# Four-column-quarter fp32 matmuls for the second half of a modulation, and a later place for two steps at the entry of a feed-forward loop

## The chip, the cores and the metric

One core of a Trainium2 chip runs the program. TensorE (PE in the profile, its weight loads PEld) multiplies, VectorE (DVE), ScalarE (ACT) and GpSimd (POOL) work element by element, SyncE (SP) issues the transfers from and to HBM. The metric is the device time in microseconds of one execution; lower is better. The program is laid out by a tile framework at build: it allots buffers and fixes the order of instructions on each engine, and at run time each engine goes through its own list in that order and waits on semaphores.

## The reference, cut to what matters

One transformer block on x of 512 tokens by 1024, in fp32, with a mixer of three kinds of heads:

```python
mod = jax.nn.silu(c) @ w_ada[l] + b_ada[l]                    # 1024 -> 6 * 1024
sh1, sc1, g1, sh2, sc2, g2 = jnp.split(mod[:, None, :], 6, axis=-1)
hn = _rms(x, norm1_g[l]) * (1 + sc1) + sh1
y = _mixer(hn, w_in[l], ...)                                  # projections, forget attention, mLSTM, block attention
x = x + g1 * (y @ w_out[l])
hn = _rms(x, norm2_g[l]) * (1 + sc2) + sh2
gate, up = jnp.split(hn @ w_gate_up[l], 2, axis=-1)
x = x + g2 * ((jax.nn.silu(gate) * up) @ w_down[l])
```

The modulation is a product of one row with a matrix of 1024 by 6144. Its "second half" below are the four parts that are not needed for the first norm: g1, sc2, sh2 and g2, 1024 columns each.

## The kernel before, in words

The first stage (to about 60 us) makes sc1 and sh1, normalizes x, transposes it and starts the first projection. The mixer stage follows (about 60 to 300 us): 70 steps, each a half row of projection products, between which a planner's queue puts the parts of the attention heads by due times written in the code. Then comes the rest of the output projection with norm 2, then the feed-forward loop (blocks of 256 of the 2816 hidden columns, q = 1 to 10, each in seven phases of a Strassen-like scheme), and the down projection in two halves.

*The modulation.* `cs` holds silu(c), 128 partitions by 8. `ada_half` (line 595) makes 512 columns: for each of 8 k, SyncE loads a tile of 128x512 of `w_ada` (tag `ast`, three buffers), and VectorE multiplies it by the column `cs[:, k]` and adds it to `acc`. The sum over partitions is left to a product with ones: `ada_row` (line 612, for g1 and g2) multiplies a full matrix of ones with `acc` into a PSUM bank of tag "t" (there are two of these) and ScalarE copies the bank to `g1b`; `ada_col` (line 619, for sc2 and sh2) multiplies four blocks of `acc` with a column of ones. g1, sc2 and sh2 are pulled by `next(ada)` once a step from step 12 on (line 1009); g2 by `next(ada2)` at every second product of the down projection (line 1352). In the profile the tiles are called g10s, g11s, sc20s, sc21s, sh20s, sh21s, g20s, g21s (loads) and g, sc, sh (sums), and g1p, g2p, sc2p, sh2p (banks).

*The entry to the feed-forward loop.* `plain(hb)` (line 1248) multiplies block 0 of the hidden columns without the scheme, for the two halves of the tokens; its bank is `fp`. `plain_glu(hb)` (line 1265) makes silu of the gate half on ScalarE (`fps`) and the product with the up half on VectorE (`A`). `operands` (line 1082) makes the scheme's operands from the normalized tokens: `operand` (line 1073) rounds a tile on ScalarE (`...h`) and subtracts on VectorE (`...l`). The last of them, s4, is a12 - a11, written over a12 (`hf<-hf`), then rounded and split (`os40h`, `os40l`, `os41h`, `os41l`). Behind these and both `plain_glu` calls stands the loop: `prepare(q, 6)` (line 1159) runs `sums` (line 1145), VectorE's sums and differences of raw weights (`r`, `r1t`), and `split` (line 1139) makes the pair `fw16h` and `fw16l` for the first product, `f1A`. The phases run in the order 1, 2, 6, 5, 7, 4, 3; for q = 1 the first two are done early, and s4 is used in phase 3. SyncE's order is the program's from line 1272 on.

Of the kernel before, what the change touches and what calls it, by code (L numbers as in the profile page):

```python
# [8 lines left out]
F32 = mybir.dt.float32  # L9
F32R = mybir.dt.float32r  # L10
I32 = mybir.dt.int32
AF = mybir.ActivationFunctionType
ALU = mybir.AluOpType
# [3 lines left out]
P = 128  # L17
SEQ = 512
NT = SEQ // P
D = 1024  # L20
# [27 lines left out]
AST = 3  # L48
# [83 lines left out]
def hybrid_block_kernel(  # L132
# [19 lines left out]
    def bank(tag, name):  # L152
        return ps.tile([P, 512], F32, tag=tag, name=name, bufs=PSB[tag])
# [438 lines left out]
        gs["em"] = em  # L592


    def ada_half(c0, name, bias):
        acc = adp.tile([P, 512], F32, tag="aacc", name=name, bufs=1)
        for k in range(8):
            s_ = adp.tile([P, 512], F32, tag="ast", name=f"{name}s{k}", bufs=AST)
            SY.dma_start(s_, w_ada_v[:, k, c0:c0 + 512])
            if k == 0:  # L600
                V.tensor_scalar(acc, s_, cs[:, 0:1], None, op0=ALU.mult)
            else:
                V.scalar_tensor_tensor(acc, s_, cs[:, k:k + 1], acc, op0=ALU.mult, op1=ALU.add)
            yield
        if bias:
            s_ = adp.tile([P, 512], F32, tag="ast", name=f"{name}b", bufs=AST)
            SY.dma_start(s_[0:1, :], b_ada[:, c0:c0 + 512])
            V.tensor_tensor(acc[0:1, :], acc[0:1, :], s_[0:1, :], op=ALU.add)
        yield
        return acc  # L610

    def ada_row(c0, dst, name):
        for hf_ in range(2):
            acc = yield from ada_half(c0 + 512 * hf_, f"{name}{hf_}", True)
            pb = bank("t", f"{name}p{hf_}")
            TE.matmul(pb, ones, acc, start=True, stop=True)
            S.activation(dst[:, 512 * hf_:512 * hf_ + 512], pb, AF.Copy)

    def ada_col(c0, name, idx):
        m = mod2[:, idx, :]  # L620
        for hf_ in range(2):
            acc = yield from ada_half(c0 + 512 * hf_, f"{name}{hf_}", False)
            pb = bank("t", f"{name}p{hf_}")
            for k in range(4):
                TE.matmul(pb[:, k:k + 1], acc[:, k * P:(k + 1) * P], ones[:, 0:1], start=True, stop=True)
            h4 = slice(4 * hf_, 4 * hf_ + 4)
            b_ = b1sc[:, 1, h4] if idx == 0 else prmT[:, 24 + 4 * hf_:28 + 4 * hf_]
            V.tensor_tensor(m[:, h4], pb[:, 0:4], b_, op=ALU.add)
        if idx == 0:
            V.tensor_tensor(m, m, prmT[:, 56:64], op=ALU.mult)  # L630

# [441 lines left out]
    def operand(name, g_, src):  # L1073

        mk = act_tile if name in ("22", "s1", "s3") else op_tile
        h_, l_ = (mk(f"o{name}{g_}{c}").rearrange("p (a b) -> p a b", a=2) for c in "hl")
        S.activation(h_, src, AF.Copy)
        V.tensor_tensor(l_, src, f32(h_), op=ALU.subtract)
        for i in range(2):
            so[name, 2 * g_ + i] = h_[:, i, :], l_[:, i, :]  # L1080

    def operands(g_):

        a11, a12 = (hfs[0, g_][:, :, i, :] for i in range(2))
        a21, a22 = (hfs[1, g_][:, :, i, :] for i in range(2))
        operand("21", g_, a21)
        operand("22", g_, a22)
        yield
        s1 = hp.tile([P, 512], F32, tag="P1", name=f"s1{g_}", bufs=SB).rearrange("p (a b) -> p a b", a=2)
        V.tensor_tensor(s1, a21, a22, op=ALU.add)  # L1090
        V.tensor_tensor(a21, a11, a21, op=ALU.subtract)
        V.tensor_tensor(a11, s1, a11, op=ALU.subtract)
        operand("s2", g_, a11)
        yield
        operand("s1", g_, s1)
        yield
        operand("s3", g_, a21)
        V.tensor_tensor(a12, a12, a11, op=ALU.subtract)
        yield
        operand("s4", g_, a12)  # L1100
        yield

    last_o(0)
# [19 lines left out]
    PHASES = (1, 2, 6, 5, 7, 4, 3)  # L1123
    BANK = {1: "A", 6: "A", 7: "A", 2: "B", 5: "C", 3: "C", 4: "D"}
    TAG = {"A": "g", "B": "s", "C": "t", "D": "s"}
    pbk, raw, wts, tmp, ffn = {}, {}, {}, {}, {}

    def wq(q, x, b):
        return gu_v[:, x, b, :, 256 * q:256 * q + 256]
# [1 line left out]
    def temp(name):  # L1131
        return act_tile(name, F32)
# [132 lines left out]
    def plain_glu(hb):  # L1265
        g_, u_ = pbank[hb]
        t_ = temp(f"fps{hb}")
        S.activation(t_, g_, AF.Silu)
        V.tensor_tensor(ffn["A"][0][:, :, 256 * hb:256 * hb + 256], u_.rearrange("p (a b) -> p a b", a=2),
                        t_.rearrange("p (a b) -> p a b", a=2), op=ALU.mult)  # L1270
# [13 lines left out]
    def some_operands(n):  # L1284
        for _ in range(n):
            for g_ in gens:
                next(g_)

    some_operands(1)
    plain(1)  # L1290
    some_operands(4)
    st.close()
    fp = ffn["fp"] = ctx.enter_context(tc.tile_pool(name="fp", bufs=1, reuse_waits="tile"))
    ffn["A"] = {q: fp.tile([P, 2, 512], F32, name=f"A{q}", padded_shape=[P, 6, 512] if q == 1 else None)
# [3 lines left out]
    raw[1, "t2"] = fp.tile([P, 4, 256], F32, tag="raw", name="r1t", bufs=RAW)  # L1298
    ffn["A"][0] = fp.tile([P, 2, 512], F32, name="A0")
    load(1)  # L1300
    for hb in range(2):
        plain_glu(hb)


    DP = [(hf_, j) for hf_ in range(2) for j in range(0, NJ, 2)]
# [24 lines left out]
    ahead = 0  # L1330
    for i, (q, ph) in enumerate(run):
        upto = todo.index(run[min(i + AHEAD, len(run) - 1)])
        while ahead <= upto:
            prepare(*todo[ahead])
            if todo[ahead] == (NQ - 1, 1):
                down_load(4)
            ahead += 1
        product(q, ph)
        after(q, ph)
# [72 lines left out]
```

## Time and profile before

| what | value |
|---|---|
| median of 3 runs | 701.18 us (701.12 to 702.85) |
| the profiled execution | 697.51 us, its span 695.8 us |
| TensorE busy | 656.3 us (94%), 4142 matmuls |
| VectorE busy | 545.4 us (78%), 1084 instructions |
| ScalarE busy | 370.3 us (53%), 757 instructions |
| GpSimd busy | 135.1 us (19%), 184 instructions |
| chain that ended last, by engine | PE 67%, DVE 21%, issue 4%, ACT 3%, DMA 3% |
| read from HBM, written | 84.15 MB, 2.10 MB |

A span is counted from the first to the last instruction of the core. Busy digits give the busy share in 40 equal slices of the span (17.4 us each), in tenths. Matmul records overlap: each is shown from its start to the end of its way through the array, so that the distance of two starts tells the rate and the length of a record does not. An fp32 call of TensorE has two records, each with a weight load; calls on operands of type fp32r, and transposes, have one. The chain of waits is followed back from the last instruction, at each step to what released it; "issue" is time in which the profile shows no wait. All instructions go through one helper, so that lines read L115 and groups are told apart by the tiles' names.

### The profile page before, as it was taken

Reading aid. Unit: us, or ns where it says so; the run is one execution under the profiler, and the core shown is the slowest. Engines: PE = TensorE matmul, PEld = TensorE weight load, DVE = VectorE, ACT = ScalarE, POOL = GpSimd, SP = SyncE. Lnnn points to the kernel's source line nnn. Section 1 sums busy time; section 2 is a strip of 40 time slices with the busy share of each in tenths; the row PEclk is TensorE's granted clock in tenths of the full one; section 3 lists DMA queues with packets and bytes.
Section 4 is the critical chain, followed back from the end, with each engine's and each line's share of the span. In section 5 each row is a group of like instructions: output and inputs, shape, how many; then the busy total and the mean of one; then the engine's idle time right before and its main releaser. Section 6 shows DMA issues by size and latency. Waiting matters only on the chain.

```text
span 695.8 us, 11756 instructions
## 1 busy us (share of the span) xinstructions
PE 656.3 (94%) x4142; PEld 597.5 (86%) x4142; DVE 545.4 (78%) x1084; ACT 370.3 (53%) x757; POOL 135.1 (19%) x184
## 2 busy tenths in 40 slices
PE   2889889999999999999996999999999999999997
PEld 2778878899999997787995999999999998788885
DVE  4998978788898989888777788877778999548313
ACT  3655536657867678645843444444545565326210
POOL 5776323442552446000000000000000000000000
PEclk9899999999999999999997999999999999999999
DMA  8963783486787667630715422233333236505101
GB/s 266 288 191 94 192 206 86 129 206 158 207 214 193 188 178 212 227 95 16 229 58 174 159 85 71 89 122 122 122 122 106 75 110 210 198 12 189 73 0 61
DMA packets 95551, 99.66 MB, mean 143 GB/s; under 512 B 8186, under 2 KB 70010, under 8 KB 95492
## 3 DMA queue, kind: packets, MB, share of 16 engines
q1 hardware_dynamic: 95492, 98.91, 48.7%
q8 instruction: 33, 0.54, 0.3%
q14 instruction: 26, 0.21, 0.1%
HBM read 84.15 MB, written 2.10 MB: 124 GB/s over the span
## 4 chain that ended last, share of the span: by engine, by line
PE 67%; DVE 21%; issue 4%; ACT 3%; DMA 3%; SPq 1%; POOL 0%; DVEq 0%; ACTq 0%; POOLq 0%
PE d L115 14%; PE F L115 7%; DVE a L115 4%; PE ol L115 4%; PE B L115 4%; PE fp L115 3%; PE mo L115 1%; PE f9A L115 1%; PE f8A L115 1%; PE f7A L115 1%; PE f6A L115 1%; PE f5A L115 1%; PE f4A L115 1%; PE f3A L115 1%; DVE cy L115 1%
## 5 line engine op out<-in xcount | busy, mean ns | idle before, releaser
L115 DVE TENSOR_TENSOR al<-A,ah 128x512 fp32r<-128x512 f32 x44 | 29.1, 685 | 18.7 <-ACT ah L115 18.7
L115 ACT ACTIVATE ah<-A 128x512 fp32r<-128x512 f32 x44 | 25.6, 620 | 33.6 <-PE d L115 33.3
L115 DVE SCALAR_TENSOR_TENSOR a<-asc,cs,a 128x128 f32<-128x128 f32 x56 | 29.7, 530 | 1.5
L115 POOL TENSOR_TENSOR a<-a,ash 128x128 f32<-128x128 f32 x40 | 23.8, 596 | 15.1 <-ACT ash L115 12.6
L115 DVE TENSOR_TENSOR r<-r,r 128x1024 f32<-128x1024 f32 x20 | 24.4, 1220 | 0.3
L115 DVE TENSOR_TENSOR fo<-d,g1b 128x512 f32<-128x512 f32 (+1 forms) x9 | 5.6, 630 | 17.9 <-PE d L115 17.8
L115 ACT ACTIVATE Fp<-Fs,Fmn 128x128 f32<-128x128 f32 (+3 forms) x24 | 12.6, 527 | 9.7 <-DVE Fmn L115 5.7
L115 POOL TENSOR_SCALAR Fp<-Fp,Fls 128x128 f32<-128x128 f32 (+2 forms) x18 | 12.0, 668 | 26.4 <-DVE Fls L115 14.2
L115 ACT ACTIVATE Bp<-Bs,Bmn 128x128 f32<-128x128 f32 (+3 forms) x24 | 12.6, 527 | 6.8 <-DVE Bmn L115 4.1
L115 POOL TENSOR_SCALAR Bp<-Bp,Bls 128x128 f32<-128x128 f32 (+2 forms) x16 | 8.7, 545 | 34.6 <-DVE Bls L115 24.9
L115 ACT ACTIVATE hf<-px,m 128x512 f32<-128x512 f32 x8 | 6.2, 776 | 17.3 <-DVE m L115 13.5
L115 ACT ACTIVATE u<-u 128x512 f32<-128x512 f32 x20 | 12.5, 626 | 2.9 <-DVE u L115 2.7
L115 DVE TENSOR_TENSOR A<-u,u 128x512 f32<-128x512 f32 x20 | 13.7, 685 | 0.0
L115 PE MATMUL pc<-ones,a 128*128 128x1 f32 x32 | 5.6, 266 | 8.5 <-POOL a L115 5.1
L115 ACT ACTIVATE smh<-E 128x512 fp32r<-128x512 f32 (+3 forms) x16 | 7.5, 470 | 11.0 <-DVE E L115 10.9
L115 POOL TENSOR_TENSOR sml<-E,smh 128x512 fp32r<-128x512 f32 (+1 forms) x8 | 8.7, 1089 | 22.3 <-ACT smh L115 22.3
L115 DVE CUSTOM_DVE_ANT_0 Bs<-Bs,mask 128x128 f32<-128x128 f32 (+3 forms) x24 | 11.6, 492 | 1.7 <-PE Bs L115 1.6
L115 PE MATMUL pc<-cs,ash 128*128 128x1 f32 x32 | 4.5, 245 | 8.9 <-DMA ash<-in_w_ada_dram 8.9
L115 DVE TENSOR_TENSOR Bptl<-Bpt,Bpth 128x128 fp32r<-128x128 f32 (+3 forms) x24 | 11.5, 484 | 1.7 <-ACT Bpth L115 1.5
L115 ACT ACTIVATE Fpth<-Fpt 128x128 fp32r<-128x128 f32 (+3 forms) x24 | 10.5, 436 | 4.4 <-PE Fpt L115 4.3
L115 ACT ACTIVATE ash<-ash,cs 128x128 f32<-128x128 f32 x40 | 12.6, 388 | 0.0
L115 PE MATMUL Bpt<-ident,Bp 128*128 128x128 f32 x60 | 10.8, 278 | 1.8 <-DVE Fyp L115 0.7
(2329 smaller groups left out, 2878.3 us busy)
## 6 DMA issues: line engine op xcount, KB each, us to landing
r<-in_w_gate_up_dram SPq DMA_DIRECT2D x40, 512.0 KB, 4.9
dr<-in_w_down_dram SPq DMA_DIRECT2D x22, 512.0 KB, 5.1
asc<-in_w_ada_dram SPq DMA_DIRECT2D x8, 512.0 KB, 5.8
ash<-in_w_ada_dram SPq DMA_DIRECT2D x8, 512.0 KB, 7.4
x<-in_x_dram SPq DMA_DIRECT2D x4, 512.0 KB, 8.2
w0s<-in_w_in_dram SPq DMA_DIRECT2D x8, 256.0 KB, 7.2
g10s<-in_w_ada_dram SPq DMA_DIRECT2D x8, 256.0 KB, 4.2
g11s<-in_w_ada_dram SPq DMA_DIRECT2D x8, 256.0 KB, 2.8
```

The costliest lines, as they stand in the source:

```text
L115: r = f(*a, **k)
```

## The change

`ada_half` is replaced by `ada_rows`, which makes 256 columns from two loads of 128x4x256 (512 KB each, two buffers). For each of the four k of a load, TensorE multiplies the tile with `cs[:, k]` spread to 32 columns, into one quarter of the partitions of a PSUM bank of tag "t"; the second load's four products add to the first's. ScalarE copies the bank, divided by 32, over the load's first block, and the products with ones are those of before, on 256 columns and into the other half of the same bank. The bias of a row is loaded to all partitions of `g1b` and added by VectorE; there is a yield behind each of the three steps of a piece.

At the entry of the loop, a12 - a11 goes to a tile of its own, and its rounding and split, together with `plain_glu(1)`, are issued behind `prepare(1, 6)`; `plain_glu(0)` stays where it was.

```diff
-    def ada_half(c0, name, bias):
-        acc = adp.tile([P, 512], F32, tag="aacc", name=name, bufs=1)
-        for k in range(8):
-            s_ = adp.tile([P, 512], F32, tag="ast", name=f"{name}s{k}", bufs=AST)
-            SY.dma_start(s_, w_ada_v[:, k, c0:c0 + 512])
-            if k == 0:
-                V.tensor_scalar(acc, s_, cs[:, 0:1], None, op0=ALU.mult)
-            else:
-                V.scalar_tensor_tensor(acc, s_, cs[:, k:k + 1], acc, op0=ALU.mult, op1=ALU.add)
+    def ada_rows(c0, name):
+        pb = None
+        for k0 in (0, 4):
+            s_ = adp.tile([P, 4, 256], F32, tag="ast", name=f"{name}s{k0}", bufs=2)
+            SY.dma_start(s_, w_ada_v[:, k0:k0 + 4, c0:c0 + 256])
             yield
-        if bias:
-            s_ = adp.tile([P, 512], F32, tag="ast", name=f"{name}b", bufs=AST)
-            SY.dma_start(s_[0:1, :], b_ada[:, c0:c0 + 512])
-            V.tensor_tensor(acc[0:1, :], acc[0:1, :], s_[0:1, :], op=ALU.add)
-        yield
-        return acc
+            if k0 == 0:
+                pb = bank("t", f"{name}p")
+            for g_ in range(4):
+                TE.matmul(pb[32 * g_:32 * g_ + 32, 0:256], cs[:, k0 + g_:k0 + g_ + 1].to_broadcast([P, 32]),
+                          s_[:, g_, :], start=k0 == 0, stop=k0 == 4)
+        acc = s_[:, 0, :]
+        S.activation(acc, pb[:, 0:256], AF.Copy, scale=1.0 / 32)
+        return acc, pb
 
     def ada_row(c0, dst, name):
-        for hf_ in range(2):
-            acc = yield from ada_half(c0 + 512 * hf_, f"{name}{hf_}", True)
-            pb = bank("t", f"{name}p{hf_}")
-            TE.matmul(pb, ones, acc, start=True, stop=True)
-            S.activation(dst[:, 512 * hf_:512 * hf_ + 512], pb, AF.Copy)
+        SY.dma_start(dst, b_ada[:, c0:c0 + D].partition_broadcast(P))
+        for i in range(4):
+            acc, pb = yield from ada_rows(c0 + 256 * i, f"{name}{i}")
+            TE.matmul(pb[:, 256:512], ones, acc, start=True, stop=True)
+            o = dst[:, 256 * i:256 * i + 256]
+            V.tensor_tensor(o, pb[:, 256:512], o, op=ALU.add)
+            yield
 
     def ada_col(c0, name, idx):
         m = mod2[:, idx, :]
-        for hf_ in range(2):
-            acc = yield from ada_half(c0 + 512 * hf_, f"{name}{hf_}", False)
-            pb = bank("t", f"{name}p{hf_}")
-            for k in range(4):
-                TE.matmul(pb[:, k:k + 1], acc[:, k * P:(k + 1) * P], ones[:, 0:1], start=True, stop=True)
...
+        for i in range(4):
+            acc, pb = yield from ada_rows(c0 + 256 * i, f"{name}{i}")
+            for k in range(2):
+                TE.matmul(pb[:, 256 + k:257 + k], acc[:, k * P:(k + 1) * P], ones[:, 0:1], start=True, stop=True)
...
+            yield
         if idx == 0:
             V.tensor_tensor(m, m, prmT[:, 56:64], op=ALU.mult)
 
@@
         operand("s1", g_, s1)
         yield
         operand("s3", g_, a21)
-        V.tensor_tensor(a12, a12, a11, op=ALU.subtract)
-        yield
-        operand("s4", g_, a12)
+        s4[g_] = temp(f"s4{g_}").rearrange("p (a b) -> p a b", a=2)
+        V.tensor_tensor(s4[g_], a12, a11, op=ALU.subtract)
         yield
@@
     some_operands(1)
     plain(1)
-    some_operands(4)
+    some_operands(3)
@@
     load(1)
-    for hb in range(2):
-        plain_glu(hb)
+    plain_glu(0)
@@
             prepare(*todo[ahead])
             if todo[ahead] == (NQ - 1, 1):
                 down_load(4)
+            if todo[ahead] == (1, 6):
+                for g_ in range(2):
+                    operand("s4", g_, s4[g_])
+                plain_glu(1)
             ahead += 1
```

## Rows read from the trace of the kernel before

**Rows 1.** The page: TensorE's busy tenths in 40 slices of the span.

```profile
PE   2889889999999999999996999999999999999997
```

**Rows 2.** Table by stage: stretch, length, busy us (instructions) of PE, PEld, DVE, ACT, POOL; granted clock, DMA.

```profile
60.00:100.00 40.00, 35.05 (x202) 31.59 (x201) 34.69 (x74) 20.02 (x42) 15.05 (x15) 0.91 0.66 168
100.00:165.00 65.00, 64.70 (x371) 56.47 (x371) 52.31 (x155) 39.77 (x120) 25.72 (x29) 1.00 0.55 143
165.00:200.00 35.00, 34.68 (x219) 33.37 (x218) 31.64 (x104) 26.17 (x73) 12.94 (x17) 1.00 0.80 208
200.00:245.00 45.00, 44.26 (x279) 42.59 (x278) 39.97 (x115) 31.80 (x87) 20.89 (x27) 1.00 0.72 195
245.00:290.00 45.00, 42.12 (x277) 37.41 (x277) 42.53 (x134) 33.35 (x85) 19.40 (x26) 1.00 0.69 195
...
560.00:597.00 37.00, 36.42 (x192) 30.59 (x191) 36.35 (x52) 21.02 (x32) 0.00 (x0) 1.00 0.59 186
...
371.70:381.80 10.10, 6.87 (x28) 6.29 (x29) 9.30 (x9) 4.29 (x5) 0.00 (x0) 0.50 0.57 169
```

**Rows 3.** Chain of waits, 60 to 292 us: shares of the stretch by line.

```profile
by line: PE F L115 21.3%; PE B L115 11.7%; issue 6.3%; PE mo L115 4.0%; DVE cy L115 3.6%; PE ms L115 3.2%; DVE Bs L115 2.3%; DVE sh L115 2.0%; DVE sc L115 2.0%; DMA sc20s<-in_w_ada_dram 1.9%; PE Fs L115 1.8%; PE Fpt L115 1.6%; DVE Bptl L115
```

**Rows 4.** Chain of waits, 560 to 597 us: shares of the stretch by line.

```profile
by line: issue 22.5%; DVE g L115 19.8%; DVE al L115 16.8%; DMA dr<-in_w_down_dram 9.0%; PE f10A L115 4.2%; DVE A L115 3.5%; DVE u L115 3.4%; DVE dw02l L115 3.3%; DVE dw014l L115 3.3%; DVE dw04l L115 3.1%; PE g2p L115 3.0%; ACT dw02h L115 2.
```

**Rows 5.** Groups by shape, DVE and ACT: count, busy us, mean ns, idle before.

```profile
L115 DVE SCALAR_TENSOR_TENSOR g<-g10s,cs,g 128x512 f32<-128x512 f32 x7 | 5.1, 726 | 0.0
...
L115 DVE SCALAR_TENSOR_TENSOR sh<-sh21s,cs,sh 128x512 f32<-128x512 f32 x7 | 6.3, 903 | 0.0
...
L115 ACT ACTIVATE Braw<-B 128x256 f32<-128x256 f32 x12 | 4.6, 382 | 1.4 <-PE B L115 1.4
```

**Rows 6.** Chain of waits, whole span: some of its longest pieces (start, us).

```profile
131.96 0.86 PE g1p L115 x2
...
384.38 2.88 PE f1A L115 x24
...
557.39 2.88 PE f10C L115 x24
...
597.01 94.35 PE d L115 x416
```

**Rows 7.** Timeline of TensorE, 131.5 to 134 us: start, us, instruction.

```profile
132.97 0.44 PE L115 MATMUL mb<-RW,sel 64*128 64x512 f32 x1
133.34 0.44 PE L115 MATMUL F<-F1w6h,hn6h 128*128 128x384 f32 x1
```

**Rows 8.** The page, DMA issues: 512 KB loads of the feed-forward weights, us to landing.

```profile
r<-in_w_gate_up_dram SPq DMA_DIRECT2D x40, 512.0 KB, 4.9
```

**Rows 9.** Waits of SyncE's queue: total us, times, longest us.

```profile
SPq L115 <- DVE g L115: 25.8, 15, 9.8
```

**Rows 10.** Timeline of TensorE, 366 to 385 us: the first product of the loop.

```profile
374.26 0.58 PE L115 MATMUL f1A<-os20h,fw16h 128*128 128x256 f32 x1 [5.53 <-ACT fw16h L115]
```

**Rows 11.** Timeline of VectorE, 358 to 383 us: in brackets idle before, releaser.

```profile
360.71 0.69 DVE L115 TENSOR_TENSOR os40l<-hf,os40h 128x512 fp32r<-128x512 f32 x1 [1.38 <-ACT os40h L115]
363.59 0.69 DVE L115 TENSOR_TENSOR os41l<-hf,os41h 128x512 fp32r<-128x512 f32 x1 [2.19 <-ACT os41h L115]
364.20 0.68 DVE L115 TENSOR_TENSOR A<-fp,fps 128x512 f32<-128x512 f32 x1
368.84 0.69 DVE L115 TENSOR_TENSOR A<-fp,fps 128x512 f32<-128x512 f32 x1 [3.96 <-PE fp L115]
369.45 2.48 DVE L115 TENSOR_TENSOR r<-r,r 128x1024 f32<-128x1024 f32 x2
...
374.11 1.22 DVE L115 TENSOR_TENSOR r<-r1t,r 128x1024 f32<-128x1024 f32 x1
375.25 1.22 DVE L115 TENSOR_TENSOR fw16l<-r1t,fw16h 128x1024 fp32r<-128x1024 f32 x1
```

**Rows 12.** Timeline of SyncE, 340 to 346 us: issues of the loop's first weight loads.

```profile
340.28 5.36 SPq L115 DMA_DIRECT2D r<-in_w_gate_up_dram  x5
```

More of the change, by code (lines that the diff above doesn't have):

```diff
@@ L619, in ada_col @@
+    def ada_row(c0, dst, name):
+        SY.dma_start(dst, b_ada[:, c0:c0 + D].partition_broadcast(P))
[5 more added lines that the diff above has]
+            yield
     def ada_col(c0, name, idx):
         m = mod2[:, idx, :]
-        for hf_ in range(2):
-            acc = yield from ada_half(c0 + 512 * hf_, f"{name}{hf_}", False)
-            pb = bank("t", f"{name}p{hf_}")
-            for k in range(4):
-                TE.matmul(pb[:, k:k + 1], acc[:, k * P:(k + 1) * P], ones[:, 0:1], start=True, stop=True)
-            h4 = slice(4 * hf_, 4 * hf_ + 4)
-            b_ = b1sc[:, 1, h4] if idx == 0 else prmT[:, 24 + 4 * hf_:28 + 4 * hf_]
-            V.tensor_tensor(m[:, h4], pb[:, 0:4], b_, op=ALU.add)
+        for i in range(4):
+            acc, pb = yield from ada_rows(c0 + 256 * i, f"{name}{i}")
+            for k in range(2):
+                TE.matmul(pb[:, 256 + k:257 + k], acc[:, k * P:(k + 1) * P], ones[:, 0:1], start=True, stop=True)
+            h2_ = slice(2 * i, 2 * i + 2)
+            b_ = b1sc[:, 1, h2_] if idx == 0 else prmT[:, 24 + 2 * i:26 + 2 * i]
+            V.tensor_tensor(m[:, h2_], pb[:, 256:258], b_, op=ALU.add)
+            yield
@@ L1125, in hybrid_block_kernel @@
     TAG = {"A": "g", "B": "s", "C": "t", "D": "s"}
-    pbk, raw, wts, tmp, ffn = {}, {}, {}, {}, {}
+    pbk, raw, wts, tmp, ffn, s4 = {}, {}, {}, {}, {}, {}
     def wq(q, x, b):
```

## The prediction

> **What bounds the kernel now.** I read the busy digits of the page first, then the table by stage, then the chain of waits of each stage, then the timeline around the places the change touches. The digits [rows 1] show TensorE at nine or more tenths nearly everywhere from slice 8 on; the one dent behind that is slice 22, around 370 us. So work that is put on TensorE is likely to be paid in full, and work taken from VectorE pays only where TensorE waits for it.
>
> The table by stage [rows 2] says where that is. In the mixer stage, 60 to 290 us, TensorE idles 4.95 us of 60 to 100, 0.30 of 100 to 165, 0.32 of 165 to 200, 0.74 of 200 to 245 and 2.88 of 245 to 290: 9.2 us in all. VectorE is busy 80 to 95% there, so it is nearly a second bound. The chain of waits of that stage [rows 3] has the modulation's own steps on it: sh 2.0%, sc 2.0% and the wait for an sc load 1.9% of 232 us, together 13.7 us. In the down projection, 560 to 597 us, TensorE is busy for 36.42 of 37 us [rows 2], although the chain [rows 4] runs through DVE g for 19.8%: VectorE is late there, but hardly later than TensorE.
>
> **Part 1, what leaves VectorE.** Eight halves lose eight steps of 128x512 each, 64 steps; 48 lie in the mixer stage, 16 around the down projection. Their rows [rows 5] go from 726 ns (g, first half) to 903 ns (sh, second half): 48 times the mean 0.81 is 39 us in the mixer, and 16 times 0.73 is 12 us in the down projection. Added on VectorE are small adds on 128x256 or 128x2 in place of smaller ones, 16 of them, none on the path. ScalarE gets 16 copies of 128x256 out of PSUM at 0.38 [rows 5], 6 us; it is the less loaded engine (26.17 of 35 us in its fullest stretch [rows 2]), and what covers a copy is the projection work that TensorE has queued. If that cover is gone, each column waits 0.4 us for its copy.
>
> What can this relief pay? At least the idle time of TensorE, 9.2 us, if the new work or the old fills it; at most that and the 13.7 us on the chain, 22.9. The upper end is far off: much of sc sits at 165 to 245 us, where TensorE is busy 34.68 of 35 and 44.26 of 45 us [rows 2], so behind a faster VectorE comes TensorE itself at once. I take 14.0: the idle time and about a third of the chain's share. In the down projection the relief is 0.6 us of idle time and a little more; I take 0.9.
>
> **Part 2, what comes to TensorE.** 16 pieces of 256 columns (12 in the mixer, 4 in the down projection), each two groups of four fp32 matmuls: 32 groups. The trace has no fp32 matmul on 32 columns of the array, so I price it from the ones-product of g1: its two records, one call of 512 columns, take 0.86 us of the chain [rows 6], 0.43 each, at granted clock 1.00 [rows 2]. For 256 columns that is 0.213 us a record and 0.427 a call. Each call loads its own weights; weight loads run beside the matmul ahead of them. The closing ones-products have as many columns as before and cost nothing new.
>
> What four quarters share is the open term, and its bounds come from the same row. Nothing: 8 records in turn, 1.71 us a group. All: two records deep, 0.43 us. In between: the calls stand in the queue as first record, second record, first, second; if starts keep that order, the second record of a quarter must wait for its first, the next quarter's first starts beside it, and a group takes five slots, 1.07 us. I take 1.07: nothing in the trace shows a matmul that overtakes another. The Trainium skill (TensorE: Matmul & The Clock Gate, "Part 3: Packing small matmuls — row/col tiling") also calls matmuls first-in first-out in start and end, which no row here contradicts; but the same part gives 2.38 times for three column tiles, by which a group would be an estimated 0.54 us and the sum would fall by 17 us.
>
> Entering and leaving a part of the array can cost too. The nearest row is a 64-row matmul of 512 columns, mb [rows 7]: the next full one starts 0.37 us after it, against 0.227 back to back (94.35 us for 416 [rows 6]), so 0.145 more. I take 0 at 32 columns, where the rows are all used, and 0.145 a group, 4.6 us for 32, as the upper end. The Trainium skill (TensorEngine Tiling (Array Packing), "Key Properties") has every change of mode drain TensorE; the mb row agrees, with these 0.145 us.
>
> TensorE also becomes the first reader of the loads. A late load now stops everything behind it in TensorE's queue, projections and transposes, where before it stopped VectorE's. The chain shows 4.4 us for such a stop (1.9% of 232) [rows 3]; I take 0, as half of a piece's loads run a piece ahead, and keep 4.4 for the range. One of the two PSUM banks tagged "t" is now held from a piece's first group to its last add, over a load that takes about 4.9 us to land at this size [rows 8]; the transposes and attention outputs then share one bank. Bounds 0 and another 4.4; I take 0 because projection products, in other banks, can be issued meanwhile.
>
> SyncE's queue: 64 loads of 256 KB become 32 of 512 KB, and two bias loads of 512 KB replace four small ones. Its waits for DVE g, 25.8 us in 15 pieces [rows 9], become waits for TensorE and ScalarE; behind them stand weight loads of later steps, as now. I cost it at nothing: loads are issued ahead of their use.
>
> So mixer: 24 groups by 1.07 are 25.6, less 14.0: +11.6 us. Down projection: 8 by 1.07 are 8.5, less 0.9: +7.6 us.
>
> **Part 3, the entry to the feed-forward loop.** TensorE idles 5.53 us until 374.26 [rows 10], so from 368.73. Its next two phases are over at 384.38; a phase takes 2.88 us at full rate [rows 6], so they could be over at 374.5: this entry costs 9.9 us. Part of it is the clock, 0.50 granted from 371.7 to 381.8 [rows 2] after the idle stretch. VectorE's queue tells why [rows 11]: os40l waits 1.38, os41l 2.19, the second product A 3.96 us (for the end of plain(1)), and only then come the weight sums r, whose loads were issued from 340.28 on [rows 12], some 29 us earlier. The change puts these three behind the sums and the first split. Without 7.53 us of waits, 1.4 us of os4 and 0.7 of A, r starts near 360, and the end of fw16l, 7.0 us behind r's start now, comes near 367, before TensorE is free. The gain lies between 0 and 9.9: the order on VectorE is fixed at build and need not be the program's (there r<-r1t,r follows the split of fw16; on VectorE it stands ahead of fw16l [rows 11]). I take 8: the margin is under 2 us. s4 is first used seven phases later; nobody waits for it.
>
> **Sum.** +11.6 + 7.6 - 8.0 = +11.2 us. The profiled execution took 697.51 us (span 695.8 and 1.7 around it), 3.7 less than the median of the runs, 701.18; a difference of microseconds carries over, so 708.7 on its scale and 712.4 by the median.
>
> **Rivals.** First, *full overlap*: the quarters run together, 0.43 us a group. For it: the outputs lie on different partitions, and nothing but the order of issue ties the calls. Against it: two records a call in one queue. Mixer 24 by 0.43 less 14.0 is -3.8, down 3.4 less 0.9 is +2.5, entry -8: -9.3 us, 691.9, faster. It decides once a group takes under about 0.72 us (32 by 0.72 equal 14.0 + 0.9 + 8.0). Second, *no overlap*: one quarter at a time, 1.71 us. For it: no row shows two matmuls streaming at once. Mixer +27.0, down +12.8, entry -8: +31.8, 733.0. Third, *the entry stays*: VectorE's queue still has A ahead of r, so the change does not do there what it says; 8 us more in each case, 720.4 from the likeliest.
>
> **How the numbers follow.** Half overlap 0.40 (712.4), full 0.35 (691.9), none 0.25 (733.0); the entry staying has 0.2 inside each. The 8-in-10 range is 688 to 733: it leaves out the upper half of no overlap and the lower tail of full overlap. The likeliest case alone has 705 to 729 (relief 5 more and the entry 9.9; or the entry 0, 4.6 for switching, 4.4 for loads). Within 0.3% (2.1 us), about what a measurement can tell from no change, are 0.06; faster has 0.33, nearly all from full overlap with the entry gained; slower 0.61.
>
> **What would show it.** The spacing of the new matmuls in the timeline: 0.21 between the quarters for half overlap, 0.43 for none, a few hundredths for full. The mixer's end against 290 us, the down projection's length, the idle time before f1A (5.53 now) and whether the clock stays at 1.00 there. The prediction is wrong if a group takes other than 1.07 us, if TensorE's queue stops at loads, or if r still follows A.

## The result, and the profile after

The changed kernel takes 727.22 us (median of 4 runs, 726.93 to 727.87), the kernel before 701.15 (698.88 to 702.85) beside it: 26.1 us slower by the medians; the ratio of the runs is 1.039 (95% interval 1.0371 to 1.041), 26.0 to 28.7 us. The forecast was 11.2 us slower, 712.4, with a range to 733: the sign was right, the size less than half of it.

The profiled execution took 727.87 us (span 726.2). That is 30.4 us more than the one of before (697.51), which lay 3.7 us under its own median; so some 4 us of any difference between the two traces is not the change's, and the sums below go by the medians.

The page after: busy time by engine, then TensorE's tenths and its granted clock in 40 slices.

```profile
PE 682.1 (94%) x4406; PEld 602.6 (83%) x4406; DVE 510.7 (70%) x1028; ACT 375.1 (52%) x769; POOL 124.8 (17%) x184
...
PE   2789899999999999989997999999999999999997
...
PEclk9999979999999999999999899999999999999999
```

VectorE has lost 35 us of work (545.4 before), TensorE gained 26 (656.3 before), and TensorE is busy 94% of the span as it was. The dent around the entry [rows 1] is still there, in slice 22 as before. The table by stage, with the columns of [rows 2]; the stretches' bounds follow the program (the end of the first projection, of the scores and so on): 183, 247, 274.5, 315 and 584.6 us are about where 165, 220, 248, 290 and 560 were before, which are not all bounds in [rows 2]. The last but one line takes in the groups of the down projection, the last one the entry:

```profile
60.00:100.00 40.00, 35.88 (x191) 32.12 (x192) 31.02 (x66) 20.11 (x43) 14.98 (x18) 0.85 0.62 161
100.00:183.00 83.00, 81.28 (x502) 63.92 (x505) 47.81 (x154) 43.58 (x130) 23.87 (x30) 0.99 0.54 151
183.00:247.00 64.00, 63.33 (x435) 53.93 (x436) 41.97 (x135) 42.01 (x113) 19.31 (x30) 1.00 0.73 199
...
274.50:315.00 40.50, 37.05 (x244) 32.94 (x243) 37.03 (x119) 30.47 (x80) 17.14 (x25) 1.00 0.60 176
584.60:622.40 37.80, 37.80 (x238) 27.84 (x237) 26.26 (x38) 20.62 (x33) 0.00 (x0) 1.00 0.55 191
396.40:406.40 10.00, 6.00 (x28) 5.41 (x29) 10.00 (x9) 3.99 (x5) 0.00 (x0) 0.66 0.53 166
```

Three things are to be seen against [rows 2]. First, VectorE is now busy 58% of 100 to 183 us where it was busy 80%, and TensorE is nearly as full as it was: 98% there (99.5% before), 99% from 183 to 247. Second, the idle time that VectorE's relief was to fill is still there: TensorE idles 4.1 us between 60 and 100 (4.95 before) and 3.5 us between 274.5 and 315 (2.88 in 248 to 290 before). Third, the entry (last line) has 6.0 us of TensorE in 10 us, at clock 0.66, against 6.87 in 10.1 at 0.50.

A group of the new matmuls, on TensorE's timeline (start, duration, instruction; a matmul's duration is long because its end is modelled, so starts are what counts):

```profile
118.63 0.33 PE L115 MATMUL F<-F1w0l,hn0h 128*128 128x384 f32 x1
118.81 0.34 PE L115 MATMUL F<-F1w0h,hn0l 128*128 128x384 f32 x1
119.08 0.64 PE L115 MATMUL g11p<-g11s,cs 128*32 128x256 f32 x8
119.64 0.44 PE L115 MATMUL F<-F1w1h,hn1h 128*128 128x384 f32 x1
119.92 0.34 PE L115 MATMUL F<-F1w1l,hn1h 128*128 128x384 f32 x1
```

Two F matmuls in a row start 0.173 us apart (118.63 and 118.81, rounded). With the group between them it is 119.64 less 118.81, 0.83 us: 0.66 more. And the F behind it needs 0.28 us until its follower, 0.11 more than usual. So a group costs 0.77 us. The other groups are alike: in the 28 of the 32 whose eight records stand together and wait for nothing, the group adds 0.65 to 0.67 us between its neighbours, in the mixer and in the down projection; the matmul behind takes 0.10 to 0.11 more where it has 384 or 512 columns, 0.06 more where it is one of some shorter ones. Inside a group, the eight records lie in two bunches: by their own start times the four first records begin 6 to 7 ns apart, the four second ones 0.24 us later, again 6 to 7 ns apart. The quarters do run together, fully; it is getting into the quarters and out that costs.

The stops that the prediction feared are few. TensorE's waits between 80 and 185 us have one for a load of the modulation:

```profile
PE sc20p L115 <- DMA sc20s<-in_w_ada_dram: 1.6, 1, 1.6
```

At the entry, VectorE's timeline (idle time and releaser in brackets) answers [rows 11], and TensorE's first product of the loop [rows 10]:

```profile
386.18 0.69 DVE L115 TENSOR_TENSOR os40l<-s,os40h 128x512 fp32r<-128x512 f32 x1 [1.38 <-ACT os40h L115]
389.06 0.69 DVE L115 TENSOR_TENSOR os41l<-s,os41h 128x512 fp32r<-128x512 f32 x1 [2.19 <-ACT os41h L115]
389.67 0.69 DVE L115 TENSOR_TENSOR A<-fp,fps 128x512 f32<-128x512 f32 x1
394.31 0.69 DVE L115 TENSOR_TENSOR A<-fp,fps 128x512 f32<-128x512 f32 x1 [3.96 <-PE fp L115]
394.92 2.48 DVE L115 TENSOR_TENSOR r<-r,r 128x1024 f32<-128x1024 f32 x2
```

```profile
399.68 0.58 PE L115 MATMUL f1A<-os20h,fw16h 128*128 128x256 f32 x1 [5.47 <-ACT fw16h L115]
```

It is the same queue as before, to the hundredth: 1.38, 2.19 and 3.96 us of waits, then r. Moving the lines in the program moved nothing on VectorE. 5.47 us of idle time, where 5.53 stood.

Between the same points of the two traces, the mixer and attention up to the loop grew by 25.5 us (fp ends at 394.21 for 368.73), the loop's entry gave back 0.8, and the down projection grew by 5.7 (from the end of f10D's last matmul to that of d's: 131.05 for 125.32).

### The profile page after: what moved, and what is told of

Same layout as the page of the kernel before. It is cut to its first block, busy times and chain, and to the rows that moved or that the text cites. A ratio compares the mean times of both kernels' runs of the same rounds, so it can differ in the third digit from the quotient of the medians.

```text
span 726.2 us, 12168 instructions
## 1 busy us (share of the span) xinstructions
PE 682.1 (94%) x4406; PEld 602.6 (83%) x4406; DVE 510.7 (70%) x1028; ACT 375.1 (52%) x769; POOL 124.8 (17%) x184
## 4 chain that ended last, share of the span: by engine, by line
PE 76%; DVE 12%; DMA 4%; ACT 3%; issue 2%; SPq 2%; DVEq 0%; ACTq 0%
PE d L115 17%; PE F L115 6%; PE B L115 6%; DVE a L115 4%; PE ol L115 3%; PE fp L115 3%; SPq L115 2%; PE ms L115 1%; PE f10A L115 1%; PE f9A L115 1%; PE f8A L115 1%; PE f7A L115 1%; PE f6A L115 1%; PE f5A L115 1%; PE f4A L115 1%
## 5 line engine op out<-in xcount | busy, mean ns | idle before, releaser
L115 DVE CUSTOM_DVE_ANT_0 Fs<-Fs,mask 128x128 f32<-128x128 f32 (+3 forms) x24 | 11.9, 497 | 11.7 <-PE Fs L115 11.6
L115 POOL TENSOR_SCALAR Fp<-Fp,Fls 128x128 f32<-128x128 f32 (+2 forms) x18 | 8.6, 479 | 35.9 <-DVE Fls L115 33.1
L115 ACT ACTIVATE Bpth<-Bpt 128x128 fp32r<-128x128 f32 (+3 forms) x24 | 10.5, 436 | 7.1 <-PE Bpt L115 6.8
L115 PEld LDWEIGHTS pc<-ones,a 128*128 128x128 f32 x32 | 5.0, 206 | 10.9 <-POOL a L115 5.8
L115 DVE TENSOR_TENSOR Fptl<-Fpt,Fpth 128x128 fp32r<-128x128 f32 (+3 forms) x24 | 11.7, 486 | 2.1 <-ACT Fpth L115 1.8
```

The costliest lines, as they stand in the source:

```text
L115: r = f(*a, **k)
```

## The experiments

The theory after the first look, A: TensorE is the bound, each group costs it 0.77 us, and taking work from VectorE pays next to nothing. The rival, B: the relief is there as forecast, but stops at late loads and at the held bank eat it. Ratios are against the kernel before, which ran beside each; its median there lay between 698.77 and 699.72 us, so differences are what to compare.

### The two halves of the change alone

Only the mixer's columns by quarter matmuls; g2 and the entry as before:

```diff
+    (ada_rows, ada_row, ada_col of the changed kernel for g1, sc2, sh2)
-    ada2 = ada_row(5 * D, g1b, "g2")
+    ada2 = ada_row_before(5 * D, g1b, "g2")
```

> Only g1, sc2 and sh2 by quarter matmuls; g2 and the entry as before (g2's sums now stand in g1b's place, and its loads come in pairs into the two larger buffers). Theory A: 24 groups at 0.75 us are 18 us, plus the 2 to 4 us that the startup and one late load took in the trace: 719 to 723. Forecast's steps: +11.6, 712.7. The rest to 727.2 is then the down projection's, 8 groups at 0.75 less its small relief, 5 to 6 us.

717.60 us against 698.77: ratio 1.0268 (1.0242 to 1.0294), 18.8 us slower: inside theory A's 18 to 22 over the kernel before, and 7 over the forecast's 11.6. That leaves 26.1 - 18.8 = 7.3 us for g2 and the entry, where 5 to 6 were expected.

Only the entry:

```diff
...
-    some_operands(4)
+    some_operands(3)
...
-    for hb in range(2):
-        plain_glu(hb)
+    plain_glu(0)
...
+            if todo[ahead] == (1, 6):
+                for g_ in range(2):
+                    operand("s4", g_, s4[g_])
+                plain_glu(1)
```

> Only the entry of the loop as in the changed kernel; the modulation on VectorE as before. Theory A (VectorE's issue order still has both products A ahead of the weight sums, so the sums start at the same distance from the end of the plain products): 0 to 1 us faster, 700 to 701. The forecast: 8 us faster, 693.2.

699.38 against 698.77: 1.0008 (0.9996 to 1.002). Nothing. VectorE's order there is that of the kernel before: os40l, os41l, both A's and then r, with waits of 1.37, 2.19 and 3.96 us.

### What the relief of VectorE is worth

First the changed kernel without its groups:

```diff
-            for g_ in range(4):
-                TE.matmul(pb[32 * g_:32 * g_ + 32, 0:256], ...)
...
-        S.activation(acc, pb[:, 0:256], AF.Copy, scale=1.0 / 32)
+        S.activation(acc, s_[:, 1, :], AF.Copy, scale=1.0 / 32)
```

> The changed kernel without the 32 groups of quarter matmuls: the loads, ScalarE's copy (now of one loaded block), the products with ones and the adds stay, so the second half of the modulation is not computed; VectorE is relieved as in the changed kernel and TensorE is not burdened. Theory A (TensorE is the bound, each group costs it about 0.75 us and VectorE's relief is worth nothing): back at the time of the kernel before, 700 to 703. Theory B (the relief of 14.0 + 0.9 us is there as forecast, and is eaten in the changed kernel by stops at late loads and at the held bank): with the entry's 0.8 us, about 685.

704.26 against 698.77: 1.0085 (1.0054 to 1.0115), slower with no group in it. Both expectations missed, A's by 1 us (its 703 lies within the interval), B's by 19 us. ScalarE's waits (who waited for whom, total, times, longest) say why it is also no clean measure:

```profile
ACT sc22s L115 <- DMA sc22s<-in_w_ada_dram: 3.2, 1, 3.2
ACT g12s L115 <- DMA g12s<-in_w_ada_dram: 3.1, 1, 3.1
ACT sc20s L115 <- DMA sc20s<-in_w_ada_dram: 3.0, 1, 3.0
```

The copy reads the load itself here, so ScalarE stops for late loads, and TensorE stands 2.6 us twice for ScalarE's results. So the relief had to be taken alone, in the kernel before, with VectorE's 64 steps left out:

```diff
+        G.memset(acc, 1.0 / 64)
...
-            if k == 0:
-                V.tensor_scalar(acc, s_, cs[:, 0:1], None, op0=ALU.mult)
-            else:
-                V.scalar_tensor_tensor(acc, s_, cs[:, k:k + 1], acc, op0=ALU.mult, op1=ALU.add)
```

> The kernel before without the 64 multiply-and-add steps of the half modulation and its bias adds on VectorE; the 256 KB loads are still made and nobody reads them, and the products with ones read a tile that GpSimd fills (the second half of the modulation is not computed). Nothing comes to TensorE or ScalarE, and no late load can stop an engine, so this is the relief alone. The forecast's Part 1: 14.9 us faster. Theory A (TensorE is the bound and the relief is worth next to nothing): 0 to 4 us faster, the most that the idle time between 60 and 100 us, 4.95 us, can give. Theory B (the relief was there and the run without groups lost it to ScalarE's waits for late loads): 9 us or more faster.

702.99 against 699.72: 1.005 (1.0033 to 1.0068), again slower, against both expectations. Nobody reads the loads any more, so nobody holds them back. The issues of sc2's first loads (in nanoseconds, then the first and last start in us), before and in this run:

```profile
L115 SPq DMA_DIRECT2D sc20s<-in_w_ada_dram x8: 346/430/584, 150.7 to 176.2; - x8
L115 SPq DMA_DIRECT2D sc20s<-in_w_ada_dram x8: 328/340/579, 126.1 to 136.0; - x8
```

The table by stage from 120 us on, two lines of before, then two of this run:

```profile
120.00:140.00 20.00, 20.00 (x110) 16.82 (x111) 14.98 (x43) 12.52 (x37) 8.95 (x10) 1.00 0.48 137
140.00:165.00 25.00, 25.00 (x158) 23.45 (x157) 20.28 (x67) 14.21 (x43) 10.28 (x13) 1.00 0.69 174
120.00:140.00 20.00, 20.00 (x109) 16.66 (x109) 11.95 (x36) 13.34 (x39) 7.35 (x8) 1.00 0.79 237
140.00:165.00 25.00, 24.05 (x151) 22.58 (x150) 14.65 (x56) 12.38 (x38) 9.25 (x14) 1.00 0.90 246
```

And TensorE's longest wait:

```profile
PE Fs L115 <- DMA K<-Fkh: 5.7, 2, 4.8
```

The DMA engines (the share next to last in a line) are busy 79 and 90% where the kernel before had 48 and 69%, and the copies of the keys come late. So the next run leaves each step on VectorE, but on one column:

```diff
+            V.tensor_scalar(acc[:, k:k + 1], s_[:, 0:1], cs[:, k:k + 1], None, op0=ALU.mult)
```

> As the run of the relief alone, but each of the 64 steps stays on VectorE as a step on one column, so that every load is still released by VectorE in its turn (the second half of the modulation is not computed). In the run before, the unread loads ran ahead and TensorE stood 4.8 us for a late copy of a key operand. If that alone made it slower, this run shows the relief itself: theory A 1 to 3 us faster than the kernel before (the idle time ahead of E and B, 1 to 2 us, and some of the 3 us ahead of A). The forecast's Part 1: 14.9 us faster. If it is slower again, relief of VectorE disturbs the order of the loads in any case.

695.63 against 699.35: 0.995 (0.9932 to 0.9968), 3.7 us faster by the medians, 3.5 by the ratio. That is the relief: 3.5 us, not 14.9, and slightly more than theory A's 1 to 3. It is not quite all of it: a step on one column still takes 0.20 us, so VectorE is busy 30 us less than before, and 35 less in the changed kernel. What TensorE waits for from 60 to 330 us, in the kernel before and in this run:

```profile
PE F L115 <- DVE Vm L115: 3.0, 1, 3.0
PE pF L115 <- DVE gtmp L115: 1.9, 1, 1.9
```

```profile
PE F L115 <- DVE Vm L115: 2.5, 1, 2.5
PE pF L115 <- DVE gtmp L115: 1.2, 1, 1.2
```

The two longest waits shrink by 0.5 and 0.7 us and the greater part of both stays. They are waits for VectorE's work ahead of the gates and of the values, and the modulation's steps are not what made most of them. Other waits grow: in all, TensorE idles 8.8 us of 60 to 330 in this run and 9.5 in the kernel before, so these traces do not place most of the 3.5 us.

### What a group costs

Each group issued twice, back to back:

```diff
+            for r_ in range(2):
                 for g_ in range(4):
```

> The changed kernel with each group of four calls issued twice back to back (scaled by 1/64 for it, so the result is the same). If a second group only streams while the array stays in quarters, it costs two records of 256 columns, 0.43 to 0.48 us, and 32 of them 14 to 15 us on top of the changed kernel: 40 to 41 us over the kernel before. If every group pays its own way in and out, 0.75 us, 24 us on top: 50 us over the kernel before.

737.55 against 699.72: 1.054 (1.0509 to 1.0571), 37.8 us over the kernel before, 11.7 over the changed one; 40 to 41 and 14 to 15 were expected, so it is a little under them, and far from 24. On the timeline, 16 records:

```profile
119.62 0.34 PE L115 MATMUL F<-F1w1h,hn1l 128*128 128x384 f32 x1
119.89 1.07 PE L115 MATMUL g11p<-g11s,cs 128*32 128x256 f32 x16
120.89 0.55 PE L115 MATMUL mo<-Vm,smh 128*128 128x130 f32 x3
```

120.89 less 119.62 less 0.173 is 1.10 us, 0.43 more than the 0.66 of a single group: a second group costs its streaming alone, 0.43 us. So of the 0.77, 0.34 us are the way in and out.

Each group replaced by one call on the whole array, with the same streaming:

```diff
-            for g_ in range(4):
-                TE.matmul(pb[32 * g_:32 * g_ + 32, 0:256], cs[:, k0 + g_:k0 + g_ + 1].to_broadcast([P, 32]),
-                          s_[:, g_, :], start=k0 == 0, stop=k0 == 4)
+            TE.matmul(pb[:, 0:256], cs[:, k0:k0 + 1].to_broadcast([P, P]), s_[:, 0, :],
+                      start=k0 == 0, stop=k0 == 4)
```

> The changed kernel with each group of four quarter calls replaced by one fp32 call on the whole array (128 columns of weights, one k of the load instead of four, so the modulation is only partly computed): the same 0.43 us of streaming as a fully overlapped group, the same loads, waits, copies and held bank, but the array never goes into quarters. If the ways in and out cost (0.75 less 0.43, some 0.3 us a group), 32 of them are 10 us less than the changed kernel: 16 us over the kernel before. If a group's cost is all streaming and the loads, waits and copies make the rest, no difference: 24 to 26 us over.

715.57 against 699.35: 1.0243 (1.0204 to 1.0282), 17.0 us over by the ratio, 9.1 less than the changed kernel. The timeline:

```profile
113.52 0.34 PE L115 MATMUL F<-F1w0h,hn0l 128*128 128x384 f32 x1
113.69 0.59 PE L115 MATMUL g11p<-g11s,cs 128*128 128x256 f32 x2
113.94 0.52 PE L115 MATMUL F<-F1w1h,hn1h 128*128 128x384 f32 x1
114.30 0.33 PE L115 MATMUL F<-F1w1l,hn1h 128*128 128x384 f32 x1
```

Here 114.30 less 113.52 holds two F matmuls and the call: 0.78 less 0.35 is 0.43 us, the streaming of two records and nothing else. So the 0.34 us belong to the quarters, not to fp32 among the others. 32 by 0.34 are 10.9 us; the runs differ by 9.1, within their intervals.

Both loads first, and one group of eight calls:

```diff
+        ld = {}
         for k0 in (0, 4):
-            s_ = adp.tile(...)
+            s_ = ld[k0] = adp.tile(...)
             SY.dma_start(s_, ...)
             yield
-            if k0 == 0:
-                pb = bank("t", f"{name}p")
+        pb = bank("t", f"{name}p")
+        for k0 in (0, 4):
+            s_ = ld[k0]
             for g_ in range(4):
```

> The changed kernel with both loads of a piece requested first and its eight calls in one group, so the array goes into quarters and out 16 times and not 32, and the bank is held only from then. From the trace, in 0.095, out 0.10 and 0.055 to 0.11 on the next matmul, about 0.27 us for a way in and out: 16 of them 4 us less than the changed kernel, 22 us over the kernel before. If the bank that a piece holds over its second load is what costs, more: 17 us or less over the kernel before. If late loads are (all of a piece's loads now come right before it), no gain or a loss: 26 or more over.

725.79 against 699.72: 1.0356 (1.0316 to 1.0396), that is 22 to 28 us over. This doesn't decide: 26 lies in it and 22 at its lower edge (12 of the 16 pieces kept their eight calls together in the trace, 12 by 0.34 are 4 us saved). The large gain that a costly bank would give, 9 us or more, is excluded; and TensorE waits 2.5 us for one piece's loads where it waited 1.6.

Last, what is left when the groups are gone but TensorE still reads each load first:

```diff
+            TE.matmul(pb[:, 0:8], s_[:, 0, 0:P], cs, start=k0 == 0, stop=k0 == 4)
```

> The changed kernel with each group of four quarter calls replaced by one fp32 call of 8 columns on the whole array (the second half of the modulation is not computed; ScalarE copies the 8 columns 32 times over). TensorE stays the first reader of every load, ScalarE's copies, the held bank, the products with ones and the adds stay; only TensorE's streaming and its ways into quarters are gone, and VectorE is relieved. If the runs so far add up (relief 3.5 us; groups 32 by 0.77, 24.6 us; measured 26.1), some 5 us remain for late loads that stop TensorE, the held bank and the copies: with the 32 short calls (0.1 us each, 3 us) it is 3 to 6 us slower than the kernel before. If the groups cost all of it and these cost nothing: 0 to 1 us faster. The forecast (relief 14.9, loads and bank 0): 12 us faster.

705.23 against 699.48: 1.0099 (1.008 to 1.0118), 5.6 to 8.3 us slower; the theory's upper end was 6. The short call itself was mis-sized:

```profile
112.32 0.33 PE L115 MATMUL F<-F1w0h,hn0l 128*128 128x384 f32 x1
112.49 0.28 PE L115 MATMUL g11p<-cs,g11s 128*128 128x8 f32 x2
112.63 0.42 PE L115 MATMUL F<-F1w1h,hn1h 128*128 128x384 f32 x1
112.89 0.34 PE L115 MATMUL F<-F1w1l,hn1h 128*128 128x384 f32 x1
```

112.89 less 112.32 less 0.35 is 0.22 us, not 0.1; 32 are 7.0. So 6.9 (by the ratio) less 7.0 plus the relief's 3.5 leaves 3.4 us for everything else that the change brings, the entry included.

### The entry, with the order enforced

VectorE's and ScalarE's instructions held to the program's order from the first A to the second, on top of the entry alone (called e4 in the expectation):

```diff
     load(1)
+    in_order["V"][0] = in_order["S"][0] = 1
     plain_glu(0)
...
                 plain_glu(1)
+                in_order["V"][0] = in_order["S"][0] = 0
```

> As e4, and VectorE and ScalarE are held to the program's order from the first product A to the second, so that the weight sums and the first split stand ahead of os40l, os41l and the second A. If the order on VectorE is all that keeps the sums back, the loop starts when TensorE is free: 8 us less than the kernel before, 693 (between 691 and 695). If the sums wait for something else (their buffers are memory that the plain products still read), the start stays near where it was: 700.

699.47 against 698.77: 1.0005 (0.999 to 1.002). Still nothing, though r now stands ahead of os40l and os41l. VectorE's and ScalarE's timelines:

```profile
371.56 0.69 DVE L115 TENSOR_TENSOR A<-fp,fps 128x512 f32<-128x512 f32 x1 [9.99 <-ACT fps L115]
372.17 2.47 DVE L115 TENSOR_TENSOR r<-r,r 128x1024 f32<-128x1024 f32 x2
```

```profile
370.93 0.60 ACT L115 ACTIVATE fps<-fp 128x512 f32<-128x512 f32 x1 [12.03 <-PE fp L115]
```

The silu fps waits 12.03 us for TensorE, to the end of the plain products, although the products that it reads were done before: in the kernel before it ran at 356.57 without a wait. The likely reason is that in this order it gets a buffer that the last plain products still read; the trace does not name buffers, so that is not shown. A waits for fps, and r stands behind A. The next run puts the sums and the first split ahead of both:

```diff
-    plain_glu(0)
+    in_order["V"][0] = in_order["S"][0] = 1
...
             if todo[ahead] == (1, 6):
+                plain_glu(0)
+                plain_glu(1)
+            if todo[ahead] == (1, 7):
                 for g_ in range(2):
                     operand("s4", g_, s4[g_])
-                plain_glu(1)
...
+        if i == 4:
+            in_order["V"][0] = in_order["S"][0] = 0
```

> The kernel before with only the entry of the loop changed: the weight sums and the first split of the loop first on VectorE and ScalarE, then both products A and silus, then s4's split, all held to this order until the fifth phase. In the run of the entry in order, the first silu's buffer was one that the plain products read to their end, and the sums stood behind it; here nothing that the plain products still read stands ahead of the sums. If that was the cause, the loop starts when the plain products end: 6 to 9 us faster than the kernel before. If the sums still start behind the plain products' end, 0 to 1 us.

694.04 against 699.72: 0.9921 (0.9891 to 0.995), 5.5 us faster by the ratio (3.5 to 7.6; 6 to 9 were expected). VectorE, and TensorE at the seam between the plain products and the loop:

```profile
362.32 1.22 DVE L115 TENSOR_TENSOR r<-r,r 128x1024 f32<-128x1024 f32 x1
...
365.98 1.23 DVE L115 TENSOR_TENSOR fw16l<-r1t,fw16h 128x1024 fp32r<-128x1024 f32 x1 [1.19 <-ACT fw16h L115]
372.33 1.29 DVE L115 TENSOR_TENSOR A<-fp,fps 128x512 f32<-128x512 f32 x2 [5.12 <-ACT fps L115]
```

```profile
371.50 0.28 PE L115 MATMUL fp<-o221h,spl 128*128 128x256 f32 x1
371.62 0.28 PE L115 MATMUL f1A<-os20h,fw16h 128*128 128x256 f32 x1
```

The sums start at 362, fw16l is done 4.4 us before TensorE is free, and f1A follows the last plain product without a gap. VectorE then idles 5.12 us ahead of the A's, while TensorE waits 3.7 us later on; so the last variant moves two more splits into that gap:

```diff
-            if todo[ahead] == (1, 6):
+            if todo[ahead] == (1, 7):
                 plain_glu(0)
                 plain_glu(1)
-            if todo[ahead] == (1, 7):
+            if todo[ahead] == (1, 4):
```

> The kernel before with the entry as in the run with the sums first, but three of the loop's sums and splits (phases 6, 5 and 7) ahead of the products A, and s4's split behind phase 4. In that run VectorE idled 5.1 us ahead of the A's and TensorE then waited 3.7 us in the first two rounds of the loop (f1A, f1D, f2A). If the splits fit into that idle time, 2 to 4 us of these come back: 8 to 9 us faster than the kernel before. If their buffers are still read by the plain products, no better than it: 5 to 6 us.

692.49 against 699.35: 0.9897 (0.9879 to 0.9914), 7.2 us faster by the ratio (6.0 to 8.5; 8 to 9 were expected), faster than both kernels; its interval overlaps that of the run with the sums first, so what the two splits add is not settled. VectorE's idle time ahead of the A's is 0.51 us, and one wait of TensorE for a weight split is left in the first two rounds:

```profile
373.07 1.29 DVE L115 TENSOR_TENSOR A<-fp,fps 128x512 f32<-128x512 f32 x2 [0.51 <-ACT fps L115]
```

```profile
PE f2A L115 <- DVE fw26l L115: 1.7, 1, 1.7
```

In its trace the last of the plain products and the last f1A start 8.6 us apart, 18.5 in the kernel before: 9.9 us less, the whole of what Part 3 said the entry costs. The rest of the loop takes 2.8 us longer (to f10D's last matmul), 2.2 of it waits of TensorE such as this one.

## Why the prediction was wrong

All three signs that it named came: a group took 0.77 us and not 1.07, TensorE's queue stopped at a load (once, 1.6 us), and r still followed A. That 727.22 lies inside its range of 688 to 733 is luck, as errors of both signs met in the sum.

| term | forecast, us | measured, us | from |
|---|---|---|---|
| 32 groups, mixer and down projection | +34.1 | +24.6 | 0.77 a group, timeline |
| relief of VectorE | -14.9 | -3.5 | steps on one column |
| entry of the loop | -8.0 | +0.6 (none) | entry alone |
| late loads, held bank, copies, the rest | 0 | +4.4 | 26.1 less the rows above, not a measurement of its own |
| sum | +11.2 | +26.1 | |

**The groups: half overlap was wrong, and so was the size.** Part 2 took 1.07 us because calls in one queue were thought to keep first and second records in turn. In the trace the four first records start within 20 ns and then the four second ones: the full-overlap rival's mechanism. The Trainium skill (TensorE: Matmul & The Clock Gate, "Part 3: Packing small matmuls — row/col tiling") gives such a set's span as one matmul and about 4 ns a further tile; the trace agrees but for the step, 6 to 7 ns, and an fp32 call has two such sets. But that rival's price, 0.43, left out the way in and out. Part 2 took 0 for it, with 0.145 as upper end from a 64-row matmul [rows 7]; it is 0.34, in pieces of 0.10 ahead of the group, 0.10 at its end and 0.11 on the next matmul, beside some 0.03 in the group. The Trainium skill (TensorEngine Tiling (Array Packing), "Key Properties") says that a change of mode drains TensorE; the trace agrees: ahead of a group, and again at its end, the next record starts 0.10 us later than streaming alone would have it. The bound was taken from a row that shows another change. The rival said it decides below 0.72 us a group, so even by its own point it fell: 0.77.

**The relief: the term that made most of the miss.** Part 1 took 9.2 us as the least, because TensorE idles that long in the mixer. That is idle time with causes of its own: the waits for Vm and gtmp, 4.9 of the 9.2 us, shrink by 1.2 when the steps are gone. The step that failed is "if the new work or the old fills it". The idle time of an engine is no lower bound of a gain; what ends each wait is. The chain's shares [rows 3] were no better: those steps stood on the chain of one execution, those of sc in stretches where TensorE itself idled only 0.3 and 0.7 us [rows 2].

**The entry: the third rival held.** Part 3 named it, that the order on VectorE need not be the program's, and it had a chance of 0.2. The step that failed is that the change puts the three waits behind the sums: the order that the build fixed came out the same. The mechanism of the 9.9 us was right: with the sums really first, 5.5 to 7.2 of them come, near the 8 that were taken, and the start of f1A is where Part 3 put it, at the end of the plain products.

**What was taken at nothing.** Loads, bank and copies together take 4.4 us by the sum (5.6 by the ratio's 27.3). The same sum leaves 2.8 us in the run with eight columns, 2.3 with the groups twice, 6.1 with the whole call and 7.3 with groups of eight, so the term is known as some 2 to 7 us. The trace shows 1.6 of it, at one late load. The cause of the rest stays open: no run here holds the bank and the loads apart, and each of these differences has an interval of 2 us or more. Nor was the pace tested: g1, sc2 and sh2 take 36 pulls, one a step, in the changed kernel and 54 before, so their loads and groups stand closer together. The granted clock does not explain it in these traces: it stands at half, the lower of its two levels, for some 20 us of the first 110 in both traces (0.91 and 0.85 in 60 to 100 us are parts of that), and for only some 10 us in the run with eight columns. The down projection came out by its parts: 8 by 0.77 are 6.2, less a relief of 0.4 (its length in the run with one-column steps, 124.92 for 125.32), 5.8; the trace shows 5.7, against 7.6 forecast.

Taking the four rows together, the errors were -9.5 (groups), +11.4 (relief), +8.6 (entry) and +4.4: the first hid more than a third of the others.

## What to carry to other kernels

Before work is moved off a busy engine, ask of each idle stretch of the bound engine what ends it, and count only those that the moved work ends; here the relief was worth 3.5 us where TensorE idled 9.2. A packed matmul is to be priced with its way into the packed mode and out, and made long: a second group behind the first cost 0.43 us, the first one 0.77. And moving lines in a program moves nothing until the queue of the engine shows it; look at the order and at the buffers it gets, and enforce the order where it matters.

## What the runs showed of the hardware

- Four fp32 calls of 256 columns on 32 columns of the array each stream as one: eight records in 0.43 us, first records 6 to 7 ns apart, the second ones 0.24 us later. Going into this mode and out cost 0.34 us in front of a matmul of 384 columns.
- An fp32 call of 8 columns on the whole array costs 0.22 us between other matmuls, half of a call of 256 columns (0.43).
- Loads that nobody reads run ahead: without VectorE's steps to hold them back, sc2's first loads were issued 25 to 40 us earlier, the DMA engines went from 48 to 79% and from 69 to 90% in two stretches, and TensorE stood 4.8 us for a copy; with the steps back on one column, that wait is gone. A reader that looks idle can be what paces a queue.
- TensorE's granted clock at the entry: 0.66 over 396.4 to 406.4 us behind 5.47 us of idle time, that is the lower of its two levels (1.2 and 2.4 GHz) for some 7 of these 10 us; in the run with the sums first, which has no such gap, it stayed at 1.00 from 366 to 396 us.
